# Turning by accumulated products: rotary sums, the two attention maps, a decay on ScalarE and 128-row score products in a decoder's mixer

## The chip, the cores and the metric

The kernel runs on one core of one Trainium2 chip. The metric is the device time of one execution in microseconds, the median of three runs. A run's profile gives the span from the first to the last instruction, a little less than the device time.

## The reference

Two decoder layers over 512 tokens of width 1024, in float32. Each layer is a half-step SwiGLU, a token mixer and a second half-step SwiGLU, each with a residual and a layer norm. What the change touches is inside the mixer:

```python
aq, ak, av, bq, bk, bv, cc = jnp.split(x @ w_in[l], IN_SPLIT_IDX, axis=-1)
aq = rope(aq.reshape(bsz, s_len, A_HEADS, 2, A_QK_DIM), positions)   # 6 heads, two maps of 32
...
def rope(x, positions):
    ...
    return jnp.concatenate([x1 * cos - x2 * sin, x2 * cos + x1 * sin], axis=-1)
def diff_attention(q, k, v, lam):
    ...
        p = jax.nn.softmax(jnp.where(causal, s, NEG_INF), axis=-1)
        attn = p[:, :, 0] - lam * p[:, :, 1]
        return jnp.einsum('bhqk,bkhd->bqhd', attn, vf)
...
bq = rope(bq.reshape(bsz, s_len, B_HEADS, HEAD_DIM), positions)       # 6 heads of 64
o_b = dilated_attention(bq, bk, bv)                                   # three dilations, one softmax
o_c = rwkv7_mixer(cc, ...)                                            # 4 heads, a state carried along the tokens
mix = jnp.concatenate([o_a, o_b, o_c], axis=-1) @ w_out[l]
```

## The kernel before, in words

Every large product is done as three products of rounded parts (`mm3`: high x high, high x low, low x high, dtype float32r); small products and transposes are in plain float32. The two SwiGLU parts (`ffn`) are products from end to end. Between them stands `Mix`, the mixer, whose work is written as some twenty streams (Python generators): `columns` (the input projection, 13 parts of 256 columns), `weights` (loading and splitting the weights), `turner`, `fetch`, `attend("A")`, `attend("B")`, the RWKV streams `decays`, `keys`, `inside`, `invert`, `scan`, `rwkv_out`, and `out` and `head` (the output projection and the start of the next SwiGLU). `Board.merge` builds one fixed order of instructions per engine: it keeps a clock per engine with a cost for each operation, and takes at each step the first stream in `RANK` whose inputs and buffers are ready by that clock. On the chip each engine runs its instructions in that order and waits for what is late. So the order on TensorE, VectorE, ScalarE, and in the queues of SyncE and GpSimd, follows from those costs, and a change of a cost moves instructions.

The path of a query or key tile: `by_token` makes 128 tokens x 256 columns in PSUM (tile `p`), VectorE multiplies by cosine (`ra`) and sine (`rb`) and adds them (`rc`); `turner` transposes the two halves of `rc` on TensorE into a PSUM tile `m`, splits it into high and low (`z`) and writes it to DRAM by SyncE (`qkA`, `qkB`); when the four tiles of a part are there, `fetch` reads them back by GpSimd's queue as `q` and `k`, per head. There are 24 such tiles in a layer (12 of group A, 12 of B).

`attend` runs over 24 units per group (three pairs of heads, two heads, four tiles of 128 queries). A unit is `scores` (products into `p`, then VectorE adds the mask and finds the extreme, then ScalarE takes the exponential into `t`), `combine`, `turn` (one transpose on TensorE for each block of 128 keys, one to four of them, 60 blocks in the 24 units; ScalarE copies them to `aT`) and `values` (product with `v` into `r`). Group A has two maps, so two tiles `t` per unit; `combine` adds the second, scaled per row by `l`, to the first on VectorE. Group B has one map, with a score product over 128 rows followed by one over 64 rows (`a[0:64]`). A float32 transpose is one matrix instruction on TensorE in the profile, a float32 product is two, so that 8 rows `r<-kr,bk` are four products. Nearly all instructions of the mixer carry one line, L504, the helper that records them; they are told apart by their tiles. `kept` holds the identity matrix.

`scan` carries the RWKV state over 8 chunks; VectorE scales the state by the decay of the next chunk (`sgm`, two instructions for each of six chunks).

Of the kernel before, what the change touches and what calls it, by code (L numbers as in the profile page):

```python
# [16 lines left out]
S = 512  # L17
# [496 lines left out]
class Mix:  # L514


    def __init__(self, tr, pool, above, p, l, dram, v_first, small):
# [7 lines left out]
        for tag, shape in (("z", (128, 2, 2, 128)), ("rc", (128, 256)), ("t", (128, S)), ("aT", (128, S)), ("bias", (128, S)),  # L525
                           ("o", (128, S)), ("u", (128, S))):
            pool.tile(list(shape), FT, name=tag, tag=tag, bufs=BUFS[tag])
# [165 lines left out]
    def by_token(self, n, kind, i):  # L693
# [5 lines left out]
        for t in range(NT):  # L699
# [19 lines left out]
            a = self.t("ra", (128, nm, 2, hd))  # L719
            b = self.t("rb", (128, nm, 2, hd))  # L720
            x4 = acc.rearrange("p (m s d) -> p m s d", s=2, d=hd)
            vec.tensor_tensor(a, x4, cos[:, t, None, None, :].to_broadcast([128, nm, 2, hd]), op=OP.mult)
            for s2 in range(2):
                vec.tensor_tensor(b[:, :, s2, :], x4[:, :, 1 - s2, :], sin[:, t, s2, None, :].to_broadcast([128, nm, hd]),
                                  op=OP.mult)
            self.drop(acc)
            c = self.get("rc", "rc", (128, 256))
            if kind == "A":
                view = lambda x: x.rearrange("p (g m) s d -> p g (s d) m", m=2)
                vec.tensor_tensor(c.rearrange("p (g d m) -> p g d m", m=2, d=32), view(a), view(b), op=OP.add)  # L730
            else:
                vec.tensor_tensor(c, a.rearrange("p m s d -> p (m s d)"), b.rearrange("p m s d -> p (m s d)"), op=OP.add)
# [8 lines left out]
    def turner(self):  # L741

        act, vec, sp = self.act, self.vec, self.sp
        for n in range(6 * NT):
# [4 lines left out]
            ps = self.acc("m", (128, 2, 128))  # L749
            for g in range(2):  # L750
                self.pe.transpose(ps[:, g, :], c[:, g * 128:(g + 1) * 128], self.tr.ident)
# [10 lines left out]
    def fetch(self):  # L762
# [3 lines left out]
        for grp in "AB":  # L766
            for hp in range(3):
                for e in range(2):
# [14 lines left out]
                    else:  # L783
                        b = self.get("x", "k2", (64, S), FR)
                        dma(a[:, 0, :], ap(d, hi, [[256 * S, 2], [S, 64], [1, S]]))
                        dma(a[:, 1, :], ap(d, hi + k, [[0, 2], [S, 64], [1, S]]))
                        dma(b, ap(d, lo + k, [[S, 64], [1, S]]))
# [312 lines left out]
    def scan(self):  # L1100
# [5 lines left out]
        for ch in range(8):  # L1106
# [28 lines left out]
            if ch < 7:  # L1135
# [12 lines left out]
                if ch < 6:  # L1148
                    sgm = self.t("sgm", (128, 2, 64), bufs=2)
                    for j in range(2):  # L1150
                        vec.tensor_scalar(sgm[:, j, :], nst[:, j, :], gam[j][:, ch + 1:ch + 2], None, op0=OP.mult)
# [6 lines left out]
    def rwkv_out(self):  # L1158

        pe, act, vec, gps, tr = self.pe, self.act, self.vec, self.gps, self.tr  # L1160
        for ch in range(8):
# [3 lines left out]
            if ch % 2 == 0:  # L1165
# [6 lines left out]
                bt = self.t("gb", (128, 256))  # L1172
# [46 lines left out]
    def attend(self, grp):  # L1219
# [6 lines left out]
        def scores(x):  # L1226
# [5 lines left out]
            x["p"] = []  # L1232
            a, b = x["qk"]
            for m in range(M):
# [3 lines left out]
                else:  # L1238
                    pe.matmul(sc[:, :nn], a[:, 0, qs], a[:, 1, :nn], start=True, stop=False)
                    pe.matmul(sc[:, :nn], a[0:64, 0, qs], b[:, :nn], start=False, stop=True)  # L1240
                t = self.get("t", "t")
# [299 lines left out]
```

## Time and profile before

| | |
|---|---|
| time, median of 3 runs | 2340.93 us (2340.63 to 2344.64) |
| the profiled execution | 2363.04 us, its span 2361.3 us |
| TensorE matmul, busy in the span | 2250.8 us (95%) |
| TensorE weight loads | 1878.7 us (80%) |
| VectorE | 1153.8 us (49%) |
| ScalarE | 804.7 us (34%) |
| GpSimd | 317.3 us (13%) |
| mean granted TensorE clock | 0.959 |

Read it so: a busy TensorE is an instruction in flight, not a TensorE at its peak, and ends of matmuls are modelled, so a steady rate is read from the starts of instructions that follow each other. The granted clock is 1 at 2.4 GHz and 0.5 at 1.2 GHz; a mean between them says for what part of a stretch each was granted. The two mixers lie at about 392 to 848 us and 1568 to 2008 us of the span.

### The profile page before, as it was taken

The page shows a single profiled execution, that of the slowest core. Times are in us where ns is not written, and L with a number is a line of the kernel's source. Part 1 is how long each engine was busy: PE and PEld are TensorE (multiplying, and loading weights), DVE is VectorE, ACT ScalarE, POOL GpSimd, SP SyncE. Part 2 cuts the span into 40 slices and gives each one's busy share as a digit, 9 for nine tenths or more (in the row PEclk, how much of TensorE's full clock was granted, in tenths as well). Part 3 has the DMA queues.
Part 4 walks back from the last instruction along what each step waited for, and adds up shares of the span by engine and source line. Part 5 has one row for each costly group of instructions (what it writes and reads, how often), then busy time and mean ns, then how long its engine had stood idle before and what let it go on. Part 6 is the DMA issues. An engine that isn't in the chain of part 4 may idle for free.

```text
span 2361.3 us, 31781 instructions
## 1 busy us (share of the span) xinstructions
PE 2250.8 (95%) x12384; PEld 1878.7 (80%) x12384; DVE 1153.8 (49%) x2535; ACT 804.7 (34%) x1559; POOL 317.3 (13%) x344
## 2 busy tenths in 40 slices
PE   9999999987899999999999999999888998999998
PEld 8888888787777788888888888886877767888886
DVE  3333346666665633332653332567665667333336
ACT  4322233434444232222332222333454443222222
POOL 1000002343221300000010000023432222000000
PEclk9999999998887899999999999998998899999999
DMA  5333344354533223322543333443545333233334
GB/s 168 99 99 97 111 137 140 99 130 86 116 95 99 89 90 91 100 96 99 169 118 107 89 92 118 144 134 91 131 93 107 96 103 117 80 98 89 98 107 152
DMA packets 265702, 258.34 MB, mean 109 GB/s; under 512 B 56314, under 2 KB 213056, under 8 KB 265552
## 3 DMA queue, kind: packets, MB, share of 16 engines
q1 hardware_dynamic: 221488, 228.20, 32.0%
q0 software_dynamic: 43488, 27.06, 5.6%
q8 instruction: 97, 1.59, 0.3%
q10 hardware_dynamic: 576, 1.05, 0.1%
q14 instruction: 53, 0.43, 0.1%
HBM read 233.85 MB, written 22.28 MB: 108 GB/s over the span
## 4 chain that ended last, share of the span: by engine, by line
PE 81%; DVE 8%; DMA 5%; issue 3%; POOL 1%; ACT 1%; SPq 0%; POOLq 0%; DVEq 0%; ACTq 0%
PE p L86 18%; PE p L87 18%; PE p L85 18%; PE p L504 13%; PE r L504 4%; PE m L504 4%; DMA k<-qkA 3%; PE r L86 2%; PE r L85 2%; PE r L87 2%; DMA k<-qkB 1%; DVE x L504 1%; DVE rs_t L504 1%; POOL q L504 0%; POOL wl L504 0%
## 5 line engine op out<-in xcount | busy, mean ns | idle before, releaser
L80 DVE TENSOR_TENSOR lo<-raw,hi 128x1024 fp32r<-128x1024 f32 x300 | 366.2, 1223 | 634.9 <-ACT hi L79 634.3
L85 PE MATMUL p<-xhi,hi 128*128 128x512 f32 (+1 forms) x1392 | 538.0, 387 | 0.5 <-ACT xhi L118 0.5
L86 PE MATMUL p<-xlo,hi 128*128 128x512 f32 (+1 forms) x1392 | 537.7, 386 | 0.7 <-DVE xlo L119 0.7
L87 PE MATMUL p<-xhi,lo 128*128 128x512 f32 (+1 forms) x1392 | 537.5, 386 | 0.0
L79 ACT CAST hi<-raw 128x1024 fp32r<-128x1024 f32 x300 | 316.0, 1055 | 589.4 <-PE p L86 263.9
L86 PEld LDWEIGHTS p<-xlo,hi 128*128 128x128 f32 x1392 | 261.8, 188 | 58.8 <-DVE xlo L119 1.1
L85 PEld LDWEIGHTS p<-xhi,hi 128*128 128x128 f32 x1392 | 261.7, 188 | 58.8 <-ACT xhi L118 1.0
L87 PEld LDWEIGHTS p<-xhi,lo 128*128 128x128 f32 x1392 | 261.8, 188 | 57.9
L504 POOL TENSOR_TENSOR wl<-wr,wh 128x512 fp32r<-128x512 f32 x152 | 203.5, 1359 | 703.2 <-ACT wh L504 653.6
L504 PE MATMUL p<-wh,xhi 128*128 128x256 f32 (+1 forms) x704 | 236.1, 335 | 2.1 <-DVE rb L504 1.9
L504 PE MATMUL p<-wh,xlo 128*128 128x256 f32 (+1 forms) x704 | 219.9, 312 | 0.2 <-DVE xlo L504 0.2
L504 PE MATMUL p<-wl,xhi 128*128 128x256 f32 (+1 forms) x704 | 219.8, 312 | 0.0
L87 PE MATMUL p<-hi,hl 128*128 128x512 f32 x528 | 205.8, 390 | 0.0
L85 PE MATMUL p<-hi,hh 128*128 128x512 f32 x528 | 205.7, 390 | 0.0
L86 PE MATMUL p<-lo,hh 128*128 128x512 f32 x528 | 205.5, 389 | 0.0
L504 PEld LDWEIGHTS p<-wh,xhi 128*128 128x128 f32 x704 | 140.6, 200 | 13.3 <-PE p L504 2.3
L504 PEld LDWEIGHTS p<-wh,xlo 128*128 128x128 f32 x704 | 140.4, 199 | 7.0 <-DVE xlo L504 1.2
L239 DVE TENSOR_TENSOR hr<-p,hr 128x512 f32<-128x512 f32 x88 | 60.9, 692 | 172.8 <-PE p L87 163.3
L504 PEld LDWEIGHTS p<-wl,xhi 128*128 128x128 f32 x704 | 141.3, 201 | 4.3 <-POOL wl L504 0.3
L240 ACT CAST hh<-hr 128x512 fp32r<-128x512 f32 x88 | 54.3, 618 | 210.1 <-DVE hr L239 200.5
L504 ACT ACTIVATE t<-t,nm 128x128 f32<-128x128 f32 (+3 forms) x144 | 80.1, 557 | 128.0 <-DVE nm L504 127.0
L86 PEld LDWEIGHTS p<-lo,hh 128*128 128x128 f32 x528 | 99.1, 188 | 20.6
(247 smaller groups left out, 3104.3 us busy)
## 6 DMA issues: line engine op xcount, KB each, us to landing
raw<-in_ffn_a_down SPq DMA_DIRECT2D x66, 512.0 KB, 3.3
raw<-in_ffn_b_down SPq DMA_DIRECT2D x66, 512.0 KB, 3.4
raw<-in_ffn_a_gate SPq DMA_DIRECT2D x44, 512.0 KB, 3.8
raw<-in_ffn_a_up SPq DMA_DIRECT2D x44, 512.0 KB, 3.9
raw<-in_ffn_b_gate SPq DMA_DIRECT2D x40, 512.0 KB, 3.9
raw<-in_ffn_b_up SPq DMA_DIRECT2D x40, 512.0 KB, 3.8
wr<-in_w_in SPq DMA_DIRECT2D x56, 256.0 KB, 3.3
wr<-in_w_in SPq DMA_DIRECT2D x24, 512.0 KB, 3.8
```

The lines of the kernel that those rows point to most:

```text
L79: nc.scalar.copy(hi, raw)
L80: (vec or nc.vector).tensor_tensor(lo, raw, hi.bitcast(FT), op=OP.subtract)
L85: mm(out, lh, rh, start=first, stop=False)
L86: mm(out, lh, rl, start=False, stop=False)
L87: mm(out, ll, rh, start=False, stop=last)
L239: nc.vector.tensor_tensor(hr, acc[1, f], hr, op=OP.mult)
L240: nc.scalar.copy(hi, hr)
L504: return call(*args, **kw)
```

## The change

Five edits, all in `Mix`. (1) `by_token` writes the cosine and the sine part into the two halves of one larger tile `rc` and no longer adds them; `turner` turns each half of the columns with two float32 products with the identity that add up in PSUM. (2) In group A `combine` no longer adds the maps; ScalarE makes a diagonal matrix `dg` (the identity scaled by row with `l`), and `turn` makes for each block of keys two float32 products that add up in PSUM: the first map by the identity, the second by `dg`. Both tiles `t` are held until then; units of up to 256 keys keep both maps in one tile. (3) The scaling `sgm` goes from VectorE to ScalarE. (4) Group B's second score product is over 128 rows: `k2` holds the low part of the keys twice and the queries' low part takes part. (5) `rwkv_out` builds its bias in the output tile `yc`.

```diff
--- before.py
+++ after.py
@@ -522,7 +522,7 @@
         for name in ("P", "omm", "omka", "gain", "nlam", "c", "gn", "wa2", "g2") + (("v1",) if l else ()):
             setattr(self, name, getattr(small, name))
         self.spill = dram.tile([NT, 128, D], FT, name=f"x_{l}")
-        for tag, shape in (("z", (128, 2, 2, 128)), ("rc", (128, 256)), ("t", (128, S)), ("aT", (128, S)), ("bias", (128, S)),
+        for tag, shape in (("z", (128, 2, 2, 128)), ("rc", (128, 512)), ("t", (128, S)), ("aT", (128, S)), ("bias", (128, S)),
                            ("o", (128, S)), ("u", (128, S))):
             pool.tile(list(shape), FT, name=tag, tag=tag, bufs=BUFS[tag])
         for tag in ("wl", "wh", "wr"):
@@ -716,20 +716,23 @@
                 continue
             yield "rc"
             cos, sin = self.c["cos" + kind], self.c["sin" + kind]
-            a = self.t("ra", (128, nm, 2, hd))
-            b = self.t("rb", (128, nm, 2, hd))
-            x4 = acc.rearrange("p (m s d) -> p m s d", s=2, d=hd)
-            vec.tensor_tensor(a, x4, cos[:, t, None, None, :].to_broadcast([128, nm, 2, hd]), op=OP.mult)
-            for s2 in range(2):
-                vec.tensor_tensor(b[:, :, s2, :], x4[:, :, 1 - s2, :], sin[:, t, s2, None, :].to_broadcast([128, nm, hd]),
-                                  op=OP.mult)
+            c = self.get("rc", "rc", (128, 2, nm, 2, hd))
+            a, b = c[:, 0], c[:, 1]
+            if kind == "A":
+                a, b = (y.rearrange("p m s d -> p (m s d)").rearrange("p (g s d m) -> p g m s d", m=2, s=2, d=16) for y in (a, b))
+                x5 = acc.rearrange("p (g m s d) -> p g m s d", m=2, s=2, d=16)
+                for s2 in range(2):
+                    vec.tensor_tensor(a[:, :, :, s2], x5[:, :, :, s2], cos[:, t, None, None, :].to_broadcast([128, 4, 2, 16]),
+                                      op=OP.mult)
+                    vec.tensor_tensor(b[:, :, :, s2], x5[:, :, :, 1 - s2],
+                                      sin[:, t, s2, None, None, :].to_broadcast([128, 4, 2, 16]), op=OP.mult)
+            else:
+                x4 = acc.rearrange("p (m s d) -> p m s d", s=2, d=32)
+                vec.tensor_tensor(a, x4, cos[:, t, None, None, :].to_broadcast([128, 4, 2, 32]), op=OP.mult)
+                for s2 in range(2):
+                    vec.tensor_tensor(b[:, :, s2, :], x4[:, :, 1 - s2, :], sin[:, t, s2, None, :].to_broadcast([128, 4, 32]),
+                                      op=OP.mult)
             self.drop(acc)
-            c = self.get("rc", "rc", (128, 256))
-            if kind == "A":
-                view = lambda x: x.rearrange("p (g m) s d -> p g (s d) m", m=2)
-                vec.tensor_tensor(c.rearrange("p (g d m) -> p g d m", m=2, d=32), view(a), view(b), op=OP.add)
-            else:
-                vec.tensor_tensor(c, a.rearrange("p m s d -> p (m s d)"), b.rearrange("p m s d -> p (m s d)"), op=OP.add)
             self.turned.append((c, kind, i, t))
             self.mark(f"turned{len(self.turned)}", self.board.ready[c.tensor.name][0])
         if kind == "v":
@@ -747,8 +750,10 @@
             yield "z", "m"
             z = self.get("z", "z", (128, 2, 2, 128), FR)
             ps = self.acc("m", (128, 2, 128))
+            h = c.shape[2] // 2
             for g in range(2):
-                self.pe.transpose(ps[:, g, :], c[:, g * 128:(g + 1) * 128], self.tr.ident)
+                for ab in range(2):
+                    self.pe.matmul(ps[:, g, :], c[:, ab, g * h:(g + 1) * h].rearrange("p m s d -> p (m s d)"), self.tr.ident, start=ab == 0, stop=ab == 1)
             act.copy(z[:, 0], ps)
             vec.tensor_tensor(z[:, 1], ps, z[:, 0].bitcast(FT), op=OP.subtract)
             self.drop(ps, c)
@@ -781,10 +786,10 @@
                         dma(a[64:96], ap(d, hi, [[2 * S, 32], [1, 2 * S]]))
                         dma(b[64:96], ap(d, lo + k, [[2 * S, 32], [1, 2 * S]]))
                     else:
-                        b = self.get("x", "k2", (64, S), FR)
+                        b = self.get("x", "k2", (128, S), FR)
                         dma(a[:, 0, :], ap(d, hi, [[256 * S, 2], [S, 64], [1, S]]))
                         dma(a[:, 1, :], ap(d, hi + k, [[0, 2], [S, 64], [1, S]]))
-                        dma(b, ap(d, lo + k, [[S, 64], [1, S]]))
+                        dma(b, ap(d, lo + k, [[0, 2], [S, 64], [1, S]]))
                     self.qkt[grp, hp, e] = a, b
                     self.mark(f"q{grp}{hp}{e}")
 
@@ -1148,7 +1153,7 @@
                 if ch < 6:
                     sgm = self.t("sgm", (128, 2, 64), bufs=2)
                     for j in range(2):
-                        vec.tensor_scalar(sgm[:, j, :], nst[:, j, :], gam[j][:, ch + 1:ch + 2], None, op0=OP.mult)
+                        act.activation(sgm[:, j, :], nst[:, j, :], AF.Copy, scale=gam[j][:, ch + 1:ch + 2])
             if cc == 3:
                 drop(yt[hf], bt[hf, 0], bt[hf, 1])
             self.chunks.append((ch, uv, st, heads, kr, vt, am))
@@ -1169,7 +1174,7 @@
                 pe.matmul(gate, self.xg[:, n * 128:(n + 1) * 128], self.g2, start=True, stop=True)
                 gg = self.t("gg", (128, 256))
                 vec.tensor_tensor(gg, gate, self.gn[:, 0], op=OP.mult)
-                bt = self.t("gb", (128, 256))
+                bt = self.yc[:, n]
                 for h in range(4):
                     hs = slice(h * 64, (h + 1) * 64)
                     vec.scalar_tensor_tensor(bt[:, hs], vt[:, h // 2, (h % 2) * 64:(h % 2) * 64 + 64], self.bon[:, n, h:h + 1],
@@ -1229,7 +1234,7 @@
             nn = max(n, 256)
             qs = slice(qt * 128, (qt + 1) * 128)
             x["l"] = self.t("l", (128, 2), bufs=8)
-            x["p"] = []
+            x["p"], x["t"] = [], []
             a, b = x["qk"]
             for m in range(M):
                 sc = self.acc("p1")
@@ -1237,8 +1242,12 @@
                     pe.matmul(sc[:, :nn], a[0:96, m, qs], b[0:96, m, :nn], start=True, stop=True)
                 else:
                     pe.matmul(sc[:, :nn], a[:, 0, qs], a[:, 1, :nn], start=True, stop=False)
-                    pe.matmul(sc[:, :nn], a[0:64, 0, qs], b[:, :nn], start=False, stop=True)
-                t = self.get("t", "t")
+                    pe.matmul(sc[:, :nn], a[:, 0, qs], b[:, :nn], start=False, stop=True)
+                if m and n <= 256:
+                    t = x["t"][0][:, n:2 * n]
+                else:
+                    x["t"].append(self.get("t", "t"))
+                    t = x["t"][-1]
                 nm = self.t("nm", (128, 1), bufs=8)
                 vec.tensor_tensor_reduce(t[:, :n], sc[:, :n], bias[:, S - n:], scale, 3e38, op0=OP.add, op1=OP.min,
                                          accum_out=nm)
@@ -1254,17 +1263,22 @@
             vec.reciprocal(r[:, :M], l[:, :M])
             if isA:
                 vec.scalar_tensor_tensor(l[:, 1:2], l[:, 0:1], self.nlam, r[:, 1:2], op0=OP.mult, op1=OP.mult)
-                vec.scalar_tensor_tensor(p[0][:, :n], p[1][:, :n], l[:, 1:2], p[0][:, :n], op0=OP.mult, op1=OP.add)
-                self.drop(p[1])
+                x["d"] = self.t("dg", (128, 128), bufs=2)
+                act.activation(x["d"], tr.ident, AF.Copy, scale=l[:, 1:2])
 
         def turn(x):
             hp, e, qt = x["id"]
             tp = self.acc("m", (128, 4, 128))
             for kb in range(qt + 1):
-                pe.transpose(tp[:, kb, :], x["p"][0][:, kb * 128:(kb + 1) * 128], tr.ident)
+                ks = slice(kb * 128, (kb + 1) * 128)
+                if isA:
+                    pe.matmul(tp[:, kb, :], x["p"][0][:, ks], tr.ident, start=True, stop=False)
+                    pe.matmul(tp[:, kb, :], x["p"][1][:, ks], x["d"], start=False, stop=True)
+                else:
+                    pe.transpose(tp[:, kb, :], x["p"][0][:, ks], tr.ident)
             x["aT"] = self.get("aT", "aT", (128, 4, 128))
             act.copy(x["aT"][:, :qt + 1], tp[:, :qt + 1])
-            self.drop(tp, x["p"][0])
+            self.drop(tp, *x["t"])
 
         def values(x):
             hp, e, qt = x["id"]
@@ -1292,7 +1306,7 @@
                     yield f"q{grp}{hp}{e}", f"v{grp}{hp}"
                     bias = self.bias
                 x["qk"], x["o"], x["ss"], x["v"] = self.qkt[grp, hp, e], o, ss, self.vt[grp, hp]
-                yield ("p1",) * M + ("t",) * M
+                yield ("p1",) * M + ("t",) * (M if qt > 1 else 1)
                 scores(x)
                 if qt == NT - 1:
                     self.drop(*x["qk"])
@@ -1306,7 +1320,7 @@
                 combine(x)
             if L2 <= i < n + L2:
                 x = units[i - L2]
-                yield x["p"][0], "m", "aT"
+                yield (x["d"] if isA else x["p"][0]), "m", "aT"
                 turn(x)
             if L3 <= i < n + L3:
                 x = units[i - L3]
```

The costs that the planner sees change with it, so the order changes from the first tile of queries on. On TensorE, around the last units of the first head of group A in layer 0 (names as above, `p_` with a number is one accumulator, each `wh`/`wl` row a piece of the input projection), before:

```order
L504 MATMUL p_4179<-k,q 128x512
L504 MATMUL p_4185<-k,q 128x512
L504 MATMUL m<-kept,t 128x128 x2
L504 MATMUL r<-v,aT 128x64
L504 MATMUL m<-kept,rc 128x128 x2
L504 MATMUL p_4212<-wh,xhi 128x256
```

and now, at the same units:

```order
L504 MATMUL p_4113<-k,q 128x384
L504 MATMUL p_4119<-k,q 128x384
L504 MATMUL m<-kept,rc 128x128 x4
L504 MATMUL m<-kept,t 128x128
L504 MATMUL m<-dg,t 128x128
L504 MATMUL p_4146<-k,q 128x512
L504 MATMUL p_4152<-k,q 128x512
```

A turned tile `rc` has gone from two transposes to four products, and a block of a unit from one transpose to a product with `kept` and one with `dg`; fewer pieces of the projection stand between the units of the first two pairs of heads.

In GpSimd's queue, ahead of the reads of group A's second pair in layer 0 (`wl` are the low parts of weights, `x` parts of the RWKV inverse, `q` and `k` the reads):

```order
 L504 TENSOR_TENSOR wl<-wr,wh 128x512 x4
-L504 TENSOR_TENSOR x_4282<-am,table 64x256 x4
-L504 TENSOR_TENSOR wl<-wr,wh 128x512 x2
 L504 DMA q<-qkA_1_2701 64x1x1024
 L504 DMA k<-qkA_1_2701 64x1x1024
 L504 DMA q<-qkA_1_2701 32x1024
 L504 DMA k<-qkA_1_2701 32x1024
-L504 TENSOR_TENSOR wl<-wr,wh 128x512 x2
-L504 TENSOR_TENSOR x_4471<-am,table 64x256 x4
+L504 TENSOR_TENSOR x_4348<-am,table 64x256 x4
```

The reads of the second pair now stand ahead of the four `x` and two `wl` that preceded them.

## Rows read from the trace of the kernel before

**Rows 1.** Windows: length, busy us (count) of PE, PEld, DVE, ACT, POOL; clock; DMA.

```profile
100.00:390.00 290.00, 290.00 (x1290) 237.23 (x1288) 120.55 (x158) 85.37 (x101) 13.13 (x14) 1.00 0.37 114
392.00:848.00 456.00, 410.03 (x2927) 354.20 (x2925) 281.43 (x865) 184.88 (x523) 137.22 (x141) 0.88 0.39 102
1568.00:2008.00 440.00, 390.61 (x2908) 335.23 (x2907) 280.60 (x867) 187.87 (x527) 136.41 (x138) 0.92 0.41 104
```

**Rows 2.** Waits of TensorE in the first mixer: total us, times, longest.

```profile
PE p L504 <- DMA k<-qkA: 20.1, 3, 10.8
...
PE m L504 <- DVE rc L504: 2.7, 1, 2.7
...
PE p L504 <- DMA k<-qkB: 0.2, 1, 0.2
```

**Rows 3.** Timeline of TensorE, 523 to 545 us: start, us, instruction, count.

```profile
524.63 0.63 PE L504 MATMUL p<-k,q 96*128 96x512 f32 x2
525.10 0.38 PE L504 MATMUL m<-kept,t 128*128 128x128 f32 x2
...
531.12 0.40 PE L504 MATMUL p<-k,q 96*128 96x256 f32 x2
531.75 0.66 PE L504 MATMUL m<-kept,t 128*128 128x128 f32 x4 [0.23 <-DVE t L504]
532.25 0.78 PE L504 MATMUL r<-v,aT 128*128 128x64 f32 x6
532.84 0.37 PE L504 MATMUL p<-wh,xhi 128*128 128x256 f32 x1
```

**Rows 4.** Timeline of TensorE, 455 to 470 us: four float32 products.

```profile
462.06 1.16 PE L504 MATMUL r<-kr,bk 64*128 64x128 f32 x8
463.15 0.39 PE L504 MATMUL p<-wh,xhi 128*128 128x256 f32 x1
```

**Rows 5.** Timeline of TensorE, 718 to 760 us: score products of group B.

```profile
726.08 0.47 PE L504 MATMUL p<-q 128*128 128x512 f32 x1
...
726.99 0.33 PE L504 MATMUL m<-kept,t 128*128 128x128 f32 x1
...
727.97 0.36 PE L504 MATMUL p<-q 128*128 128x256 f32 x1
...
728.57 0.70 PE L504 MATMUL m<-wa,c 128*128 128x256 f32 x2
```

**Rows 6.** Groups of instructions, first mixer: count, busy us, mean ns, idle before.

```profile
L504 DVE TENSOR_TENSOR rc<-ra,rb 128x256 f32<-128x256 f32 x24 | 14.8, 618 | 0.8
L504 DVE SCALAR_TENSOR_TENSOR t<-t,l 128x128 f32<-128x128 f32 (+3 forms) x24 | 14.7, 611 | 0.8
...
L504 ACT ACTIVATE junk<-r 128x64 f32<-128x64 f32 x48 | 15.1, 314 | 24.2 <-DVE o L504 19.5 <-DVE rs_y L504 3.9
...
L504 DVE TENSOR_TENSOR rb<-p,table 128x128 f32<-128x128 f32 x48 | 11.4, 279 | 0.0
...
L504 DVE TENSOR_TENSOR ra<-p,table 128x256 f32<-128x256 f32 x24 | 10.0, 416 | 4.8 <-PE p L504 4.7
...
L504 DVE TENSOR_SCALAR sgm<-st,gam 128x64 f32<-128x64 f32 x12 | 6.0, 710 | 0.0
```

**Rows 7.** Timeline of GpSimd, 480 to 800 us, ahead of group A's second pair.

```profile
527.66 3.23 POOL L504 TENSOR_TENSOR x<-am,table 64x256 f32<-64x256 f32 x4
535.97 2.51 POOL L504 TENSOR_TENSOR wl<-wr,wh 128x512 fp32r<-128x512 f32 x2 [5.08 <-PE r L504]
```

**Rows 8.** DMA issues, 500 to 730 us: count, KB each, median us to landing.

```profile
qkB<-z SPq DMA_DIRECT2D x12, 256.0 KB, 2.5
...
k<-qkB POOLq DMA_DIRECT2D x6, 128.0 KB, 9.6
```

**Rows 9.** Windows late in group B: busy us, granted clock (columns of rows 1).

```profile
722.00:732.00 10.00, 9.96 (x60) 7.53 (x58) 7.90 (x38) 6.59 (x25) 1.13 (x2) 0.97 0.43 148
733.00:756.00 23.00, 23.00 (x97) 18.54 (x96) 8.87 (x41) 7.68 (x28) 3.36 (x5) 0.50 0.27 93
```

## The prediction

> **What bounds the kernel now.** I read the windows first, because the share of busy time over the whole span mixes two kinds of stages. In a SwiGLU stretch TensorE is busy for all of its 290 us at a granted clock of 1.00, and nothing of this change lies there. In the two mixers it is busy for 410.0 of 456 us and 390.6 of 440 us, VectorE for 281 us in each, ScalarE for 185 and 188 us [rows 1]. So of 896 us of mixer TensorE is idle for 95.4 us, and VectorE, from which the change takes work, is idle for over a third of it. The second thing to see there is the clock: 0.88 and 0.92, which is 54.7 us and 35.2 us of full-clock time not given (456 x 0.12, 440 x 0.08).
>
> Then the waits of TensorE in the first mixer. The largest by far is for the keys of group A that come back from DRAM, 20.1 us in three waits; the wait for the added rotary tile, which the change ends sooner, is one of 2.7 us [rows 2]. What sets the end of a mixer is therefore TensorE's own row of instructions, which runs in a fixed order, plus a few waits for memory. VectorE's additions are mostly off that path.
>
> **The change part by part, for one layer.** I need the time of a transpose and of a float32 product on TensorE, from start to start. Four transposes of 128x128 take 532.25 - 531.75 = 0.50 us, 0.125 us each; three float32 products 64 wide take 0.59 us, 0.197 us each [rows 3]. Four float32 products 128 wide take 1.09 us, 0.27 us each, with the step from and back to products over 128 rows included [rows 4]. The new products are 128 wide over all 128 rows, a case the trace hardly shows: between 0.197 and 0.27 us. I take 0.25, two instructions at the transposes' pace.
>
> *Turning the maps.* A block was one transpose and becomes two products: 2 x 0.25 - 0.125 = 0.375 us. 60 blocks: +22.5 us (16.1 with 0.197, 25.2 with 0.27).
>
> *Turning the rotary tiles.* Two transposes become four products: 4 x 0.25 - 2 x 0.125 = 0.75 us. 24 tiles: +18.0 us (12.9 to 20.2).
>
> *Score products over 128 rows.* Now group B's pair takes 726.99 - 726.08 = 0.91 us at 512 keys and 0.60 us at 256 [rows 5]. Group A's pair, whose 96 rows have no 64-row product in it, takes 0.47 us at 512 and 0.40 us at 256 [rows 3]. If the second product over 128 rows goes as A's does, a unit saves 0.44 or 0.20 us, and at 384 I take the middle, 0.32: 6 x 0.44 + 6 x 0.32 + 12 x 0.20 = 6.9 us. Bounds: nothing, and 8.9 us if 256 keys go at half the time of 512 (0.60 - 0.235 = 0.365 us). I take -6.9.
>
> *VectorE and ScalarE.* VectorE loses 24 additions of 618 ns, 24 of 611 ns and 12 scalings of 710 ns, 38 us of busy time; group A's 12 rotary tiles cost 4 x 279 = 1116 ns in place of 416 + 2 x 279 = 974 ns, +1.7 us [rows 6]. Little of this is on the path: the 2.7 us wait for `rc` is cut by one addition, and a few shorter ones elsewhere go. I take -2 us, bounds 0 and -5. ScalarE gets 24 diagonals and 12 scalings; at the price of the nearest row, 314 ns, that is 11.3 us [rows 6] on an engine busy for 185 us of 456, so I cost it at nothing. What hides a diagonal is the one unit that lies between `combine` and `turn`; without that cover a turn waits 0.31 us for it, 7.5 us in 24.
>
> *What moves.* In GpSimd's queue the reads of A's second pair stood behind 3.2 us of `x` and 2.5 us of `wl`, the last of them after a 5.1 us wait for TensorE [rows 7]. They now stand ahead of these. That can shorten the 10.8 us wait [rows 2]; I take -4 us, bounds 0 and -10.8. Group B loses cover: its write and read-back take 2.5 + 9.6 = 12.1 us [rows 8]. Between the last turned tile of B's first part and its first score product the order had 84 projection pieces, 19 transposes and 20 value products, among others; it now has 78 pieces, 4 value products and 16 small ones. At half of A's 512-key product, 0.1175 us, 78 pieces are 9.2 us, some 11 in all, under the 12.1. Its other two parts come out alike (72 pieces and 12 products; for the third about half the value products and transposes are gone). I take +5 us for the three, bounds 0 and +15. The doubled `k2` reads go in the same packets' time as the `q` reads beside them, and cost nothing as long as those are awaited too. The bias in `yc` moves no engine's work: nothing.
>
> Sum for a layer: 22.5 + 18.0 - 6.9 - 2 - 4 + 5 = +32.6 us, two layers +65.2 us. The profiled execution was 2363.0 us, with 1.7 us around its span, and would be 2428. The median of the three runs is 22.1 us below it; the same step on it gives 2340.9 + 65.2 = **2406 us**. With all terms at their ends a layer gets 20.1 - 5 - 10.8 = +4 us to 45.4 + 15 = +60 us; ends do not all meet, so I give this case 2380 to 2432.
>
> A rule weighs against the change more than my rows do. By rows 3 and 4 a float32 product is at most 0.27 us and so about two transposes of 0.125. The Trainium skill, TensorE: Matmul & The Clock Gate (Terms, on the XBUS), says that transpose mode is four times as fast for float32. Read as a ratio to a product that gives 0.5 us a product. The row next to it, 0.27 us, contradicts it for products over 64 rows; no row has 128 rows at that width.
>
> **The rivals.**
>
> *The clock comes back (faster).* Late in group B TensorE is busy for all of 23 us at a clock of 0.50, right after a stretch busy for 9.96 of 10 us at 0.97 [rows 9]; both consist of transposes and narrow products. If the new full-width products keep the clock at 1.00 where transposes did not, up to 89.9 us of the two mixers come back: 2340.9 + 65.2 - 89.9 = 2316 us. It decides from 65.2 of 89.9, 73% of what is lost. For it speaks that this loss isn't idleness there; against it, that the waits for keys remain. Chance 0.20.
>
> *It hides (same).* TensorE idles 95.4 us; if the added products fall into that, the time stays at 2341. Against it: they stand in front of what is waited for (a tile is turned before it is written and read back), so a wait moves and doesn't shrink. Chance 0.08.
>
> *The clock or the waits get worse (slower still).* With fewer projection pieces between the units of A's first pairs, TensorE waits on ScalarE's exponentials, and the three B reads cost their +15: 2406 + 2 x 12.5 = 2431 us. Chance 0.17.
>
> *A product is four transposes.* At 0.5 us: 60 x 0.875 + 24 x 1.75 - 6.9 = +87.6 us, with the other terms (-2 - 4 + 5) +86.6 us a layer, 2340.9 + 2 x 86.6 = 2514 us. Chance 0.02.
>
> **How the numbers follow.** The forecast has the rest, 0.53. A change within 0.2%, 4.7 us, can't be told from none here. Slower: 0.53 + 0.17 + 0.02 = 0.72; same: 0.07, faster: 0.21, as some of the hidden case falls a little below. The range leaves about one in ten on each side: 2318, near where the clock returns in full, to 2438, just past the worse case.
>
> **What would show it.** In the changed profile eight rows `m<-kept,rc` in a turn would span 0.9 to 1.1 us from start to start, and the pair `p<-q`, `p<-k,q` at 512 keys under 0.5 us; TensorE busy in the mixers up by some 30 us each, VectorE down by some 36 us; waits for `k<-qkB` of a few us where there were 0.2 [rows 2]. I am wrong if the mixers don't grow: then either the granted clock there has risen to above 0.97, or VectorE's work was on the path in a way that the waits don't tell.

## The result: 3.0% slower

The changed kernel takes 2411.7 us (four runs, 2406.4 to 2414.1) against 2340.8 us before (four runs), a ratio of 1.0296 with a 95% interval of 1.0279 to 1.0313. That is +71 us, where +65 was reckoned. The profiled execution of the changed kernel is one of its four, 2406.4 us with a clock of 0.968; that of the kernel before had a clock of 0.959 and was 22 us above its median, whose later runs have 0.970. So the two spans differ by 43 us only, and stages are compared by work and waits, and times by medians. A run over 1.5% above the fastest of its kernel is left out of the ratios below, which concerns five of the twelve runs of read_cost and no other.

The windows of the changed kernel, for the same SwiGLU stretch and its two mixers (columns as in [rows 1]):

```profile
100.00:390.00 290.00, 290.00 (x1289) 237.20 (x1288) 120.37 (x158) 85.33 (x101) 13.56 (x14) 1.00 0.37 114
392.00:857.00 465.00, 416.88 (x3252) 373.93 (x3251) 254.56 (x817) 194.47 (x559) 136.51 (x141) 0.93 0.40 102
1577.00:2052.00 475.00, 419.72 (x3233) 373.16 (x3233) 252.99 (x820) 199.06 (x564) 135.53 (x138) 0.92 0.39 98
```

The SwiGLU is untouched. In each mixer TensorE has some 325 more instructions, VectorE is busy for 255 and 253 us in place of 281, and the idle time of TensorE is 48.1 and 55.3 us in place of the 46.0 and 49.4 us of [rows 1].

The timeline of TensorE, with the new products (start, us, instruction, count). First two tiles of rotary parts, the second with a transpose behind it, then one unit of three blocks, then a pair of group B at 256 and at 512 keys:

```profile
635.90 1.16 PE L504 MATMUL m<-kept,rc 128*128 128x128 f32 x8
636.99 0.45 PE L504 MATMUL r<-uv,bt 128*64 128x64 f32 x8
...
738.91 1.05 PE L504 MATMUL m<-kept,rc 128*128 128x128 f32 x8
739.80 0.27 PE L504 MATMUL m<-kept,t 128*128 128x128 f32 x1
739.91 1.00 PE L504 MATMUL r<-v,aT 128*128 128x64 f32 x8
```

```profile
575.67 0.38 PE L504 MATMUL m<-kept,t 128*128 128x128 f32 x2
575.89 0.39 PE L504 MATMUL m<-dg,t 128*128 128x128 f32 x2
576.11 0.39 PE L504 MATMUL m<-kept,t 128*128 128x128 f32 x2
576.34 0.39 PE L504 MATMUL m<-dg,t 128*128 128x128 f32 x2
576.56 0.39 PE L504 MATMUL m<-kept,t 128*128 128x128 f32 x2
576.78 0.39 PE L504 MATMUL m<-dg,t 128*128 128x128 f32 x2
577.01 0.56 PE L504 MATMUL r<-v,aT 128*128 128x64 f32 x4
```

```profile
742.10 0.36 PE L504 MATMUL p<-q 128*128 128x256 f32 x1
742.30 0.28 PE L504 MATMUL p<-k,q 128*128 128x256 f32 x1
742.42 0.60 PE L504 MATMUL m<-kept,o 128*128 128x128 f32 x4
...
745.76 0.48 PE L504 MATMUL p<-q 128*128 128x512 f32 x1
746.08 0.39 PE L504 MATMUL p<-k,q 128*128 128x512 f32 x1
746.30 0.39 PE L504 MATMUL p<-wh,xhi 128*128 128x512 f32 x1
```

Read from start to start: four products of a tile take 1.09 us in the one place and 0.89 us in the other; six products of a unit take 577.01 - 575.67 = 1.34 us, 0.223 us each; the transpose at 739.80 takes 0.11 us, so a product is two transposes of 0.112 us; group B's pair takes 0.32 us at 256 keys and 0.54 us at 512, where it took 0.60 and 0.91 [rows 5].

The waits of TensorE in the first mixer, then four lines of the second. Of the kernel before follow the queries of group B in the first mixer and the keys of group A in the second:

```profile
PE p L504 <- DMA k<-qkA: 19.6, 3, 10.5
PE p L504 <- DMA q<-qkB: 7.7, 2, 4.8
...
PE p L504 <- DMA k<-qkB: 3.2, 3, 1.5
```

```profile
PE p L504 <- DMA k<-qkA: 15.8, 2, 10.4
PE m L504 <- DVE rc L504: 9.5, 2, 9.1
PE p L504 <- DMA q<-qkB: 7.8, 2, 4.5
...
PE p L504 <- DMA k<-qkB: 3.2, 3, 2.4
```

```profile
PE p L504 <- DMA q<-qkB: 0.2, 1, 0.2
```

```profile
PE p L504 <- DMA k<-qkA: 21.3, 3, 9.2
```

Group B's reads are now waited for, in the two mixers for 10.9 and 11.0 us, where in the first it was 0.2 us for its keys [rows 2] and as much for its queries. The wait for group A's keys has not become shorter in the first mixer; in the second it has, from 21.3 to 15.8 us, and there a wait of 9.1 us for a rotary tile is new.

### The profile page after: what moved, and what is told of

It reads as the page before. It is cut to its first block, busy times and chain, and to the rows that moved or that the text cites. A ratio compares the mean times of both kernels' runs of the same rounds, so it can differ in the third digit from the quotient of the medians.

```text
span 2404.6 us, 33009 instructions
## 1 busy us (share of the span) xinstructions
PE 2285.8 (95%) x13032; PEld 1935.7 (80%) x13032; DVE 1098.4 (46%) x2439; ACT 825.1 (34%) x1631; POOL 316.1 (13%) x344
## 4 chain that ended last, share of the span: by engine, by line
PE 82%; DMA 7%; DVE 7%; issue 3%; ACT 1%; POOL 1%; SPq 0%; POOLq 0%; DVEq 0%; ACTq 0%
PE p L86 18%; PE p L85 18%; PE p L87 18%; PE p L504 13%; PE r L504 5%; PE m L504 5%; DMA k<-qkA 3%; DMA k<-qkB 2%; PE r L87 2%; PE r L86 2%; PE r L85 2%; DVE rs_t L504 1%; DVE x L504 1%; DMA td<-tt 1%; DMA qkA<-z 1%
## 5 line engine op out<-in xcount | busy, mean ns | idle before, releaser
L504 PE MATMUL p<-wh,xhi 128*128 128x256 f32 (+1 forms) x704 | 229.3, 326 | 0.9 <-ACT xhi L504 0.6
L504 PEld LDWEIGHTS p<-wh,xhi 128*128 128x128 f32 x704 | 137.8, 196 | 10.7 <-ACT xhi L504 3.1
L87 PEld LDWEIGHTS p<-hi,hl 128*128 128x128 f32 x528 | 99.1, 188 | 20.5
```

What stands on the lines that cost most here:

```text
L87: mm(out, ll, rh, start=False, stop=last)
L504: return call(*args, **kw)
```

## The experiments

The theory: TensorE's own row of instructions sets the end of a mixer, so each product added there is paid for, and VectorE's relief is worth next to nothing. The rivals: the loss comes from the order that the planner makes of the new costs, and from the waits in it; or the clock does it. Each kernel was run against the kernel before on the same chip, whose median was 2340.5 to 2342.2 us. "Clock" is the median of the granted clock over the kernel's runs; before it is 0.970. Where the planner's costs change, it makes a new order; rows128, decay_same_order and turn_same_order keep TensorE's order row for row, and after_old_costs is meant to come nearer to it.

The last three columns split the span of the profiled execution. "Idle" is the span without TensorE's busy time. "Clock" is an estimate of the time lost to the half clock, the span times one minus the mean granted clock. "Rest" is what then remains, the work at full clock. They belong to one execution, not to the median, so they are compared with each other and not with the second column.

| kernel | median us | ratio (95%) | clock | idle | clock, us | rest |
|---|---|---|---|---|---|---|
| before | 2340.8 | | 0.970 | 110 | 97 | 2154 |
| the changed kernel | 2411.7 | 1.0296 (1.0279, 1.0313) | 0.968 | 119 | 77 | 2209 |
| u_maps | 2377.4 | 1.0141 (1.0113, 1.0169) | 0.970 | 124 | 66 | 2178 |
| u_rotary | 2394.5 | 1.0213 (1.0185, 1.0240) | 0.965 | 127 | 79 | 2180 |
| small_edits | 2348.5 | 1.0018 (0.9998, 1.0038) | 0.970 | 126 | 75 | 2146 |
| turn_products | 2390.1 | 1.0199 (1.0163, 1.0235) | 0.966 | 122 | 69 | 2185 |
| turn_same_order | 2361.2 | 1.0077 (1.0054, 1.0099) | 0.968 | 101 | 68 | 2188 |
| rows128 | 2337.8 | 0.9982 (0.9959, 1.0005) | 0.970 | 119 | 68 | 2149 |
| decay_act | 2371.6 | 1.0132 (1.0101, 1.0163) | 0.959 | 118 | 97 | 2154 |
| decay_same_order | 2346.7 | 1.0012 (0.9987, 1.0038) | 0.970 | 110 | 65 | 2159 |
| dve_back | 2447.2 | 1.0445 (1.0415, 1.0475) | 0.960 | 135 | 88 | 2210 |
| after_old_costs | 2387.4 | 1.0181 (1.0146, 1.0215) | 0.971 | 95 | 79 | 2216 |
| read_cost | 2361.1 | 1.0038 (1.0006, 1.0069) | 0.951 | 83 | 111 | 2160 |
| read5_rows | 2317.5 | 0.9882 (0.9848, 0.9916) | 0.972 | 97 | 65 | 2152 |

### u_maps: the maps added on VectorE again

```diff
@@ attend, against the changed kernel
-                x["d"] = self.t("dg", (128, 128), bufs=2)
-                act.activation(x["d"], tr.ident, AF.Copy, scale=l[:, 1:2])
+                vec.scalar_tensor_tensor(p[0][:, :n], p[1][:, :n], l[:, 1:2], p[0][:, :n], op0=OP.mult, op1=OP.add)
+                self.drop(p[1])
...
-                    pe.matmul(tp[:, kb, :], x["p"][0][:, ks], tr.ident, start=True, stop=False)
-                    pe.matmul(tp[:, kb, :], x["p"][1][:, ks], x["d"], start=False, stop=True)
+                pe.transpose(tp[:, kb, :], x["p"][0][:, kb * 128:(kb + 1) * 128], tr.ident)
```

> The changed kernel with edit 2 undone: the two maps are added on VectorE again and a block is turned by one transpose. If TensorE's own work sets the mixer's end, the 60 blocks a layer at 0.375 us come off: 2412 - 45 = 2367 us (2361 to 2380 by the bounds of the term). If the loss lies in the changed order and in the waits for keys read back, which stay, the time hardly moves: 2395 to 2412. If taking the additions from VectorE gave something back, less than 45 comes off.

Measured 2377.4 us: turning the maps costs 34 us on top of the rest, of 45 reckoned. The larger part of the theory's figure is there; some of it is given back. In the table the rest falls by 31 us, and the idle time rises by 5.

### u_rotary: the rotary parts added on VectorE again

```diff
@@ by_token and turner, against the changed kernel
...
+                vec.tensor_tensor(c, a.rearrange("p m s d -> p (m s d)"), b.rearrange("p m s d -> p (m s d)"), op=OP.add)
...
-                for ab in range(2):
-                    self.pe.matmul(ps[:, g, :], c[:, ab, g * h:(g + 1) * h].rearrange("p m s d -> p (m s d)"), self.tr.ident, start=ab == 0, stop=ab == 1)
+                self.pe.transpose(ps[:, g, :], c[:, g * 128:(g + 1) * 128], self.tr.ident)
```

> The changed kernel with edit 1 undone: VectorE adds the rotary parts, two transposes per tile. If TensorE's own work decides, 24 tiles a layer at 0.75 us come off: 2412 - 36 = 2376 us (2371 to 2386). If order and waits decide, 2395 to 2412.

Measured 2394.5 us: 17 us come off, half of the 36, at the edge of what order and waits alone would give. The work did go: the rest is 29 us less. But TensorE idles 9 us more. With the maps undone as well (small_edits) the same edit is worth 2377.4 - 2348.5 = 29 us. The two edits together cost 63 us.

### small_edits: edits 3, 4 and 5 on the kernel before

> The kernel before with edits 3, 4 and 5 alone: the decay on ScalarE, group B's score products over 128 rows, the bias in yc. By the term for the score products, 6.9 us a layer less of TensorE's work: 2341 - 14 = 2327 us, a little less if the scalings waited on the path. If the second product costs the same over 128 rows, or the order moves against it, 2341.

Its diff is the three lines of edit 4, the one of edit 3 and the one of edit 5 as shown ahead. Measured 2348.5 us, no gain. The 14 us that the score products save are not at the end: the rest is 8 to 13 us less than in the two profiles of TensorE's old order with the old score products (before, decay_same_order), and the idle time is 16 us more.

### rows128: edit 4 alone

```diff
-                        b = self.get("x", "k2", (64, S), FR)
+                        b = self.get("x", "k2", (128, S), FR)
...
-                        dma(b, ap(d, lo + k, [[S, 64], [1, S]]))
+                        dma(b, ap(d, lo + k, [[0, 2], [S, 64], [1, S]]))
...
-                    pe.matmul(sc[:, :nn], a[0:64, 0, qs], b[:, :nn], start=False, stop=True)
+                    pe.matmul(sc[:, :nn], a[:, 0, qs], b[:, :nn], start=False, stop=True)
```

> The kernel before with edit 4 alone, score products over 128 rows in group B; TensorE's order stays as it was, row for row. If TensorE's work sets the end: 2 x 6.9 us less, 2342 - 14 = 2328 us. If the time saved in group B is given back as waits for its queries and keys to be read: 2342, with that much more idle time ahead of score products.

TensorE's order is the same row for row, and still only 3.5 us of 14 arrive, within what can be told from none. TensorE idles 119 us where it idles 110 in both profiles of the same order with 64 rows, so most of the saving comes back as waiting. Two of its waits in the first mixer, and then the reads of group B's keys:

```profile
PE p L504 <- DMA k<-qkA: 17.9, 3, 10.3
...
PE p L504 <- DMA k<-qkB: 6.3, 3, 4.2
```

```profile
k<-qkB POOLq DMA_DIRECT2D x6, 256.0 KB, 10.7
```

The wait for group B's keys is 6.3 us where it was 0.2 [rows 2] and, in decay_same_order, 0.9. A read lands no sooner because TensorE gets to it sooner, and here it also lands later: the doubled read is of 256 KB and takes 10.7 us to land, where 128 KB took 9.6 [rows 8]. How much of the wait is the one and how much the other was not tried.

### decay_act and decay_same_order: edit 3 alone, in a new order and in the old one

```diff
@@ scan (decay_act)
-                        vec.tensor_scalar(sgm[:, j, :], nst[:, j, :], gam[j][:, ch + 1:ch + 2], None, op0=OP.mult)
+                        act.activation(sgm[:, j, :], nst[:, j, :], AF.Copy, scale=gam[j][:, ch + 1:ch + 2])
@@ decay_same_order: the planner is given VectorE's cost for it
+                        act.activation(sgm[:, j, :], nst[:, j, :], AF.Copy, scale=gam[j][:, ch + 1:ch + 2], as_=("vec", 0.07 + 64 / 960.0))
```

> The kernel before with edit 3 alone, the state's decay on ScalarE. The planner's order moves with it. If the scalings stood on the path: up to 12 x 0.7 us a layer less, 2325 us. If they did not and the moved order is as good: 2342. If the moved order is what cost the three small edits their gain: 2350 to 2360.

> The kernel of decay_act (the state's decay on ScalarE), but the planner is told VectorE's cost, so that the order is the order before. If the moved order, and the clock granted with it, made the 30 us: 2341 us with the granted clock back at 0.970. If the scaling on ScalarE is dear in itself: 2371.

Measured 2371.6 and 2346.7 us. The same work costs 25 us more in another order. TensorE's idle time differs by 8 us in the two profiles, 118 and 110 us; the clock differs more, 0.959 against 0.970. Of 2370 us, 0.011 is 26 us. The scaling itself, on either engine, is worth nothing that can be told.

### turn_products and turn_same_order: TensorE's work alone

```diff
@@ turn, against the kernel before
-                pe.transpose(tp[:, kb, :], x["p"][0][:, kb * 128:(kb + 1) * 128], tr.ident)
+                pe.matmul(tp[:, kb, :], x["p"][0][:, kb * 128:(kb + 1) * 128], tr.ident, start=True, stop=True)
@@ turn_same_order: with the transposes' cost for the planner
+                pe.matmul(tp[:, kb, :], x["p"][0][:, kb * 128:(kb + 1) * 128], tr.ident, start=True, stop=True, as_=("pe", 2 * 128 / 2400.0 + 0.003))
```

> The kernel before, where every transpose of an attention block, of both groups, is a float32 product with the identity; nothing is taken from VectorE. This is TensorE work alone, 120 blocks a layer. If a product is two transposes and TensorE's work decides: 120 x 0.125 x 2 = +30, 2371 us. If such work hides in TensorE's idle time: 2341. If products keep the clock up where transposes do not: below 2341. If a product is four transposes: 2431.

> The kernel of turn_products (each transpose of an attention block a float32 product), but the planner is told the transposes' old cost, so that every engine's order is the order before, row for row. This is the price of TensorE's own work without any move. At two transposes a product: 120 x 0.112 to 0.125 x 2 = 27 to 30 us, 2341 + 28 = 2369 us. If the 48 us of turn_products are all such work: 2389. If it hides in TensorE's idle time: 2341.

(`as_` is an argument added to the helper that records the operations; it changes only the cost that the planner notes.) With every engine's order as before, 240 products in place of transposes cost 20.6 us (12.6 to 23.2 by the interval). At the 0.112 us that the timelines show it is 27 us of work, so between half and nine tenths of it reach the end; TensorE's idle time falls from 110 to 101 us, which fits the part that does not. With the order that the planner makes of the true costs, the same work costs 48 us, and TensorE idles 122 us. So the price of TensorE's work was right, a part of it hides, and a moved order can cost as much again, here mostly as waits.

### dve_back: VectorE's work put back

```diff
@@ by_token and combine, against the changed kernel
+            c2 = c.rearrange("p k m s d -> p k (m s d)")
+            vec.scalar_tensor_tensor(c2[:, 0], c2[:, 1], 0.0, c2[:, 0], op0=OP.mult, op1=OP.add)
             self.turned.append((c, kind, i, t))
...
+                vec.scalar_tensor_tensor(p[0][:, :n], p[1][:, :n], 0.0, p[0][:, :n], op0=OP.mult, op1=OP.add)
                 x["d"] = self.t("dg", (128, 128), bufs=2)
```

> The changed kernel with VectorE's removed work put back as additions of a zero multiple in place (24 of 256 columns and 24 of up to 512 keys a layer), ahead of the turning; the output stays what it was. If taking this work from VectorE gave nothing: 2412 us. If it gave back part of what TensorE pays (the two turning edits cost 63 us by the runs where 81 were reckoned): some 2430. If VectorE were the bound, 29 us a layer: 2470.

Measured 2447.2 us, 35 us over the changed kernel. In the profiled executions the rest is the same (2209 and 2210 us), the idle time is 17 us more and the clock costs 11 us more. The two waits of TensorE that grew most, over the whole span:

```profile
PE m L504 <- DVE xlo L504: 17.7, 8, 4.7
...
PE m L504 <- DVE o L504: 9.2, 3, 3.8
```

They were 11.5 and 3.3 us in the changed kernel. All waits that end with VectorE come to 55 us, where they came to 39. So the relief, with the order that goes with it, was worth more than the 4 us reckoned, by some 16 us of waits. The clock of these runs is 0.960, which by the medians explains some 20 of the 35 us (0.968 - 0.960, of 2447). How much is the delay itself and how much the order that it makes, this run doesn't tell.

### after_old_costs: the changed kernel in an order nearer the old one

```diff
@@ against the changed kernel: what the planner is told
+                act.activation(x["d"], tr.ident, AF.Copy, scale=l[:, 1:2], as_=("vec", 0.07 + n / 960.0))
...
+                    pe.matmul(tp[:, kb, :], x["p"][0][:, ks], tr.ident, start=True, stop=False, as_=("pe", 128 / 2400.0 + 0.0015))
+                    pe.matmul(tp[:, kb, :], x["p"][1][:, ks], x["d"], start=False, stop=True, as_=("pe", 128 / 2400.0 + 0.0015))
```

(The products of `turner` and the decay are told the same way.)

> The changed kernel with the planner told the old costs for the products that turn, for the diagonal and for the decay: the same work, in an order nearer the one before (not the same, since the tiles t are held longer). If the 71 us are TensorE's work: 2405 to 2420. If the moved order made part of it: 2380 to 2400. If the order that knows the true costs is the better one: above 2420.

Measured 2387.4 us, 24 us less than the changed kernel with all of its work. The moved order is a part of the loss; the order that knows the products' true cost is the worse one. By the medians 7 us of the 24 are the clock, 0.971 against 0.968; in the profiled executions (2391.7 and 2406.4 us) the clock costs much the same, and TensorE idles 95 us in place of 119. Its waits for the reads, over the whole span:

```profile
PE p L504 <- DMA k<-qkA: 29.2, 6, 6.7
...
PE p L504 <- DMA q<-qkB: 10.8, 2, 5.5
...
PE p L504 <- DMA k<-qkB: 3.2, 3, 1.4
```

These are 43 us; in the changed kernel they are 35.4, 15.5 and 6.4, together 57 us.

### read_cost and read5_rows: the planner told of later reads

```diff
@@ Board.note
-            end += 2.0
+            end += 9.0 if name == "pool" else 2.0
@@ read5_rows: 5.0 in place of 9.0, with the lines of rows128
```

> The kernel before with one number of the planner's changed: a transfer issued by GpSimd is taken to land 9 us after its issue and transfer time instead of 2 us, near the 8 to 19 us of the trace. The work is the same, only the order moves. If the waits for keys of about 20 us a layer come from an order that expects them too early: 2342 - 20 to - 40, 2302 to 2322. If there is no other work to put ahead of them: 2342. If the planner then delays the attention: above 2350.

> The kernel before with edit 4 (score products over 128 rows) and the planner told 5 us in place of 2 for transfers issued by GpSimd. With 9 us the waits fell and the granted clock fell too. If half the step keeps the clock: 2341 - 6 - 12 = 2323 us. If the clock falls again: 2340 to 2360.

With 9 us the waits for keys are gone: TensorE idles 83 us, 27 us less than before. But the kernel is no faster (ratio 1.0038), since its clock is 0.951. Its runs scatter from 2336 to 2385 us, and the slowest have the lowest clock: 0.965 in the fastest, 0.940 in the slowest. Two windows of its first mixer, and below them what TensorE did in the second of them:

```profile
660.00:676.00 16.00, 14.46 (x110) 10.88 (x111) 9.49 (x53) 10.23 (x40) 4.32 (x6) 1.00 0.29 56
677.00:723.00 46.00, 45.33 (x176) 35.81 (x177) 18.23 (x91) 17.40 (x64) 3.22 (x6) 0.50 0.25 81
```

```profile
L504 PE MATMUL r<-v,aT 128*128 128x64 f32 x60 | 14.1, 402 | 0.0
L504 PE MATMUL m<-kept,t 128*128 128x128 f32 x29 | 8.9, 435 | 0.6 <-DVE gb L504 0.6
L504 PE MATMUL p<-k,q 64*128 64x256 f32 (+2 forms) x8 | 5.3, 659 | 0.0
L504 PE MATMUL p<-q 128*128 128x256 f32 (+2 forms) x8 | 5.1, 641 | 0.0
L504 PE MATMUL p<-wh,xhi 128*128 128x512 f32 x6 | 4.4, 732 | 0.8 <-ACT xhi L504 0.8
```

For 46 us TensorE is busy for 45.3 and runs at 1.2 GHz. What it does there are group B's units one after the other, with few wide products between. The clock fell at 676 us, behind two waits, and rose at 724 us, in a row of wide products without a wait, whose starts are 0.43 us apart ahead of the rise and 0.29 us behind it:

```profile
675.67 0.63 PE L504 MATMUL m<-kept,o 128*128 128x128 f32 x4 [1.54 <-DVE rs_t L504]
677.07 0.79 PE L504 MATMUL p<-wh,xhi 128*128 128x512 f32 x1 [0.78 <-ACT xhi L504]
...
723.46 0.63 PE L504 MATMUL p<-wh,xhi 128*128 128x512 f32 x1
723.89 0.45 PE L504 MATMUL p<-wl,xhi 128*128 128x512 f32 x1
724.18 0.40 PE L504 MATMUL p<-wh,xlo 128*128 128x512 f32 x1
```

With 5 us and the 128-row score products the kernel takes 2317.5 us, 1.2% less than before, at a clock of 0.972, the best time of all kernels here. The waits of its first mixer:

```profile
PE m L504 <- DVE xlo L504: 12.3, 6, 4.1
PE p L504 <- DMA k<-qkA: 4.9, 1, 4.9
...
PE p L504 <- DMA k<-qkB: 2.7, 1, 2.7
```

The two waits for keys are 7.6 us where they were 20.3 [rows 2], while that for `xlo` has grown from 6.8 us; TensorE idles 97 us in place of 110, and the clock has kept. The 5 us without the 128 rows were not tried.

## Why the prediction was right, and where two terms were not

**The bound** was read rightly: TensorE's row of instructions, with few waits, sets a mixer's end. turn_same_order shows it with nothing else changed. How the 71 us come about is best read beside decay_same_order, which has TensorE's old order at a usual clock (0.972) and takes what the kernel before takes. TensorE's busy time there and in the changed kernel, of spans of 2334.6 and 2404.6 us:

```profile
PE 2224.7 (95%) x12384; PEld 1855.7 (79%) x12384; DVE 1145.8 (49%) x2511; ACT 809.8 (35%) x1583; POOL 317.3 (14%) x344
```

```profile
PE 2285.8 (95%) x13032; PEld 1935.7 (80%) x13032; DVE 1098.4 (46%) x2439; ACT 825.1 (34%) x1631; POOL 316.1 (13%) x344
```

The 70 us between these spans are, by the table, some 50 us of work, 9 us of idle time and 12 us of clock.

**Turning the maps and the rotary tiles.** A product was put at 0.25 us and took 0.223; a tile's four took 0.89 and 1.09 us, about the forecast's 0.9 to 1.1. By 0.223 us and 0.112 us for a transpose, the maps are 60 x (2 x 0.223 - 0.112) x 2 = 40 us and the tiles 24 x (4 x 0.223 - 2 x 0.112) x 2 = 32 us of work, 72 where 81 was reckoned. Together the two edits cost 63 us as measured (small_edits against the changed kernel), relief and moved order included.

**Score products over 128 rows.** The saving on TensorE is as forecast: 0.37 us a pair at 512 keys and 0.28 at 256, against 0.44 and 0.20, though the pair at 512 keys takes 0.54 us, not the under 0.5 that was named as a sign. The step that failed is the next one, that what TensorE saves there arrives at the end: 3.5 of 14 us did, and idle time took most of the others' place (rows128). The doubled reads, which were put at nothing, land 1.1 us later (10.7 against 9.6 us) and were waited for.

**VectorE's relief** was mis-sized: -2 us a layer, from the idle time in front of TensorE. With its additions put back, TensorE idled 5 us more (u_maps), 9 us more (u_rotary) and 17 us more (dve_back, both additions), the last of these nearly all in waits for VectorE; each of the three has an order of its own, so the price of the relief alone is not shown. A list of waits shows only where an engine stands still now; it doesn't show how near the other waits are behind. VectorE's busy time fell by 27 us a mixer, not by 36; a small part of the difference is that the sum counted 12 scalings at 710 ns, 8.5 us, where their row has 6.0 us busy [rows 6]. TensorE's busy time rose by 7 and 29 us in the two mixers in place of some 30 each; the first of these is small because the kernel before had a clock of 0.88 there and the changed kernel 0.93.

**What moves.** +1 us a layer was taken as the sum of a shorter wait for group A and longer ones for group B. The longer ones came as some 11 us in each mixer, in the forecast's 0 to 15; the shorter one came in the second mixer alone, 5.5 us. For two layers TensorE's waits for these reads rose from 43 to 57 us, +15 in place of +2. after_old_costs has the same work with 43 us of them, and is 24 us faster.

**Why the sum is so near.** That 65 lies beside 71 is in part luck. The two turning edits cost 63 us, some 16 less than their terms with the relief and the moved reads (81 - 4 + 2 = 79), and the small edits cost 8 us (2348.5 - 2340.8) where -14 was reckoned. The two misses nearly cancel. Split the other way, the work came out smaller than the forecast's 67 us (57 by the rates above, 72 less 15 for the score products; some 50 by the table), and idle time and clock, some 20 us together, filled the gap.

**The rivals.** The clock did not come back: 0.968 in the changed kernel's runs against 0.970, and 0.966 in turn_products. The work did not hide, or only in part (turn_same_order). A product is not four transposes: 0.223 us is two of 0.112. The ratio that I read out of the Trainium skill, TensorE: Matmul & The Clock Gate (Terms), does not hold for these products.

What stays open: how the order moves the clock. decay_act and decay_same_order have the same work, idle times 8 us apart, and clocks of 0.959 and 0.970; which part of the order does it was not tried. In the other two pairs of orders, turn_products with turn_same_order and the changed kernel with after_old_costs, the profiles differ by idle time, 21 and 24 us, and hardly by the clock. Open too is the share of the doubled reads in the wait for group B's keys.

## What to carry to other kernels

Where one engine is busy nine tenths of a stage, moving work onto it from one that is a third idle costs most of its time (here 63 of 72 us, relief and order included), while the relief on the other side must be measured, not read from the list of waits. A saving on the path counts only up to the next transfer that must land: look for its issue, its landing and what work stands between. Where a planner sets the order, try an edit with the order held as it was: the edit and the order are two changes. Here one number in the planner, with edit 4, was worth 23 us (read5_rows), where edit 4 alone gave 3.5.

## What the runs showed of the hardware that was not expected

TensorE ran at half clock through stretches in which it was all but always busy: 46 us in read_cost (busy 45.3, clock 0.50) and 23 us in the kernel before [rows 9]. They consist of transposes and narrow float32 products with few wide ones. Both began behind short waits, 1.54 and 0.78 us in read_cost and 0.73 us in the kernel before, and the half clock then stayed through work with hardly a wait (0.7 us of idle time in the 46, none in the 23). The new products with `kept` and `dg` were seen at full clock too, in a stretch of the changed kernel that was all busy:

```profile
574.00:584.00 10.00, 10.00 (x94) 9.55 (x94) 4.99 (x31) 9.23 (x33) 3.75 (x3) 1.00 0.19 54
```

But 29 pieces of the projection, 256 wide, stand in that stretch, so it does not show that the products keep the clock up.

The sum of idle time does not account for the clock here: in read_cost idle time fell by 27 us and the clock from 0.970 to 0.951. A score product over 64 rows behind one over 128 cost 0.60 us a pair at 256 keys, and 0.32 us once both went over 128 rows, so the step to 64 rows cost nearly half of the pair.
